# Turning x on VectorE and carrying it through DRAM at the stage boundaries of a two-layer encoder trunk

## The chip, the cores and the metric

The kernel runs on one core of one Trainium2 chip, in one launch. The metric is the device time of the whole program in microseconds (us). Engines are named as in the profile: PE is TensorE's matmul, PEld its weight load, DVE is VectorE, ACT is ScalarE, POOL is GpSimd, SP is SyncE, which here issues nearly all DMAs from one queue, in order.

## The reference

The model is a trunk of two layers over x of shape (1, 256, 1024) in float32, with a memory of 256 x 1024. Cut to what matters here:

```python
for i in range(2):
    x = x + 0.5 * swiglu(rmsnorm(x, ffn1_norm[i]), ffn1_w_gate[i], ffn1_w_up[i], ffn1_w_down[i])
    h = rmsnorm(x, mix_norm[i])
    q_s, k_s, v_s, q_m = split(h @ w_in[i])              # 768, 768, 768, 256 columns
    k_m, v_m = split(rmsnorm(mem, mem_norm[i]) @ w_mem_kv[i])
    o_m = memory_attention(...)                          # 4 heads of 64 over 256 memory rows
    o_s = chunked_rel_attention(...) if i == 0 else diff_attention(...)   # 12 heads, or 6 pairs of heads
    x = x + concat(o_s, o_m) @ w_out[i]
    x = x + 0.5 * swiglu(rmsnorm(x, ffn2_norm[i]), ffn2_w_gate[i], ffn2_w_up[i], ffn2_w_down[i])
# swiglu(h) = (silu(h @ w_gate) * (h @ w_up)) @ w_down, with w_gate, w_up 1024 x 2816 and w_down 2816 x 1024
```

## The kernel before, in words

**Stages.** Feed-forward 1, mixer, feed-forward 2, twice: six stages with five boundaries between them. x stays in SBUF as two blocks of 128 tokens (`xs[tb]`, `tb` 0 and 1), each handled in two halves of 512 columns (`hf`).

**Arithmetic.** A float32 product is made of three matmuls in a reduced form: every operand is split into hi (a rounded copy, ScalarE) and lo (the rest, VectorE), and `dense` (lines 370 to 393) issues hi x hi (L383), x hi x weight lo (L386) and x lo x weight hi (L389), each 128 x 128 by 512 columns. One call of `dense` is three matmuls.

**Weights.** They come in chunks of 128 x 2048 float32 (1 MB). `loader` fills `raw` buffers (three), `split_hi` (L302) and `split_lo` (L314) split them by quarters of 512 columns into hi and lo buffers (four of each, `NHL`). A raw buffer is free again when lo is made, a hi/lo pair when all eight `dense` calls on the chunk are done. A gate/up group of a feed-forward stage has two chunks, one for each half of the 1024 inputs; there are 11 groups. Each `w_down` chunk serves 256 of the 2816 inner columns; there are 11 of these too.

**x for the next stage.** `prep_half` makes from a half of x the turned, gain-multiplied operands: TensorE turns four 128 x 128 squares into a PSUM tile (`xtp`, `turn`, L396), VectorE multiplies by the norm's gain (`y`, L427), ScalarE makes hi (`xh`, L430), VectorE lo (`xl`, L432). The sum of squares runs beside it (`square`, L441); the factor it gives is applied after the matmuls. `finish` (from L460) adds the stage's result to x (L466 after feed-forward, L469 after a mixer) and calls `prep_half`, half after half, for one block.

**Feed-forward.** `ffn` runs the gate/up groups; `evac` takes each group's result: silu on ScalarE (L491), the product on VectorE (L494), and then turns it for the down product without TensorE: VectorE turns 32 x 32 squares (L503, two instructions for each block and group), SP writes the tile `hb` to a DRAM tile `hd` (L508) and reads it back in four pieces in the other block order (`hr`, L514); hi and lo follow (L521, L523). The down product keeps four PSUM banks (2 blocks x 2 halves). The first 8 of 11 chunks (`SPLIT = NG - 3`) run chunk by chunk over all four banks; the last three run bank by bank, so that block 0 half 0 is complete first, then block 0 half 1, block 1 half 0, block 1 half 1, and `finish` can begin on the early ones. I call these four stretches the tail's quarters.

**Order of the groups.** Group 0 of a stage (but the very first) runs block 0 with both chunks and then block 1; later groups run chunk by chunk, with both blocks on each.

**Mixer.** `proj` runs five projections, each block 0 then block 1: q and k of four heads, v (512 columns), q and k twice more, and last the rest of v with the memory's queries. Eight attention units (`unit`) run beside them as their inputs come. The output product has four chunks, two run chunk by chunk, two bank by bank as above. Before the first mixer the memory is prepared (`memory_prep`, started in the first feed-forward stage after down chunk 6: TensorE turns `mtp`, ScalarE L630, VectorE L635), and its key/value projections for both layers (`memory_kv`) run ahead of the mixer's own.

**Who sets the order.** The order on every engine and queue is fixed when the program is written, by a planner (`Flow`) with its own clock and cost for each instruction. A piece of work is a generator that yields the planned time at which its next step is ready. The two weight splits are idle work: they get in where the planner believes the engine to be free within 0.4 us, or when TensorE has already come to the chunk:

```python
yield lambda: flow.free["A"] <= flow.now + SLACK or i <= at[0] + AHEAD
```

At run time the engines follow that order and wait on semaphores; an instruction that waits holds up everything behind it on its engine or queue.

## Time and profile before

| | |
|---|---|
| time, median of 3 | 975.2 us (974.78 to 975.77) |
| profiled execution | 975.12 us, span from first to last instruction 973.3 us |
| granted TensorE clock | 1.00 throughout |
| busy, share of the span | PE 99%, PEld 81%, DVE 69%, ACT 56%, POOL 6% |
| DMA | 200.9 MB, mean 206 GB/s |
| turns of x on TensorE (xtp, L396) | 96 in 24 groups of four, 280 ns each |
| turns of the activations on VectorE (L503) | 176, 289 ns each |

A row of the groups of instructions reads: line, engine, operation, output<-inputs, shapes, xcount | busy us, mean ns. A row of the timeline or of an engine's list reads: start us, duration us, engine, line, operation, output<-inputs, count, and in brackets the idle time of the engine before it and what ended that. A row of the stretches reads: from:to, length, then for each of PE, PEld, DVE, ACT and POOL the busy us and instruction count, granted clock, DMA share, GB/s. PE's busy time has modelled ends; the starts of the weight loads (PEld) show TensorE's pace.

First matmuls of the stages behind the five boundaries: memory projections 193.77, feed-forward 2 320.57, feed-forward 1 of layer two 502.02, the second mixer between 683 and 684.2, feed-forward 2 of layer two 789.12 us.

### The profile page before, as it was taken

How to read it: one execution, taken by the hardware profiler on the slowest of the kernel's cores; microseconds unless marked ns; L12 is line 12 of the kernel's file. 1: busy time of each engine (PE TensorE's matmuls, PEld its weight loads, DVE VectorE, ACT ScalarE, POOL GpSimd, SP SyncE). 2: the span in 40 equal slices, each digit the busy share in tenths (PEclk: the TensorE clock that was granted, in tenths of full speed). 3: DMA queues.
4: the chain of work that ended last, by engine and by line, in shares of the span. 5: the costliest groups of instructions: out<-in, count | busy, mean ns of one | idle time of the engine just before them, and what ended most of it. 6: DMA issues, size and time to landing. Idle time of an engine off the chain costs nothing.

```text
span 973.3 us, 13393 instructions
## 1 busy us (share of the span) xinstructions
PE 964.6 (99%) x4576; PEld 791.3 (81%) x4576; DVE 675.7 (69%) x1485; ACT 542.4 (56%) x1159; POOL 60.1 (6%) x65
## 2 busy tenths in 40 slices
PE   9999999999999999999999999999999999999998
PEld 7888888887777888888888888888787788888886
DVE  6776675887777866666476676644989886676641
ACT  6554544766685655445445555443677764555540
POOL 0000000022210000000000000000344100000000
PEclk9999999999999999999999999999999999999999
DMA  9989766475525567887648887764641369788641
GB/s 289 306 242 270 257 225 206 162 260 173 174 87 173 163 209 223 242 263 242 235 124 252 250 252 237 253 207 136 207 140 50 125 199 284 235 251 254 226 130 44
DMA packets 164447, 200.90 MB, mean 206 GB/s; under 512 B 9433, under 2 KB 140058, under 8 KB 164378
## 3 DMA queue, kind: packets, MB, share of 16 engines
q1 hardware_dynamic: 164378, 200.04, 65.5%
q8 instruction: 36, 0.59, 0.3%
q14 instruction: 33, 0.27, 0.1%
HBM read 187.42 MB, written 12.58 MB: 205 GB/s over the span
## 4 chain that ended last, share of the span: by engine, by line
PE 91%; DVE 5%; ACT 1%; DMA 1%; issue 0%; SPq 0%; ACTq 0%
PE gu L383 16%; PE gu L386 16%; PE gu L389 16%; PE acc L386 9%; PE acc L389 9%; PE acc L383 9%; PE pj L389 3%; PE pj L383 3%; PE pj L386 3%; DVE lo L314 2%; PE xtp L396 1%; PE S L983 1%; PE AV L1064 1%; PE kv L389 1%; PE kv L386 1%; PE kv L383 1%
## 5 line engine op out<-in xcount | busy, mean ns | idle before, releaser
L314 DVE TENSOR_TENSOR lo<-raw,hi 128x512 fp32r<-128x512 f32 x656 | 416.5, 684 | 161.5 <-ACT hi L302 161.3
L302 ACT CAST hi<-raw 128x512 fp32r<-128x512 f32 x656 | 365.4, 618 | 241.3 <-PE gu L389 117.9
L389 PE MATMUL gu<-hi,xl 128*128 128x512 f32 x704 | 274.3, 390 | 0.0
L383 PE MATMUL gu<-hi,xh 128*128 128x512 f32 x704 | 274.1, 389 | 0.0
L386 PE MATMUL gu<-lo,xh 128*128 128x512 f32 x704 | 274.0, 389 | 0.0
L389 PEld LDWEIGHTS gu<-hi,xl 128*128 128x128 f32 x704 | 132.2, 188 | 27.5
L383 PEld LDWEIGHTS gu<-hi,xh 128*128 128x128 f32 x704 | 132.2, 188 | 27.3
L386 PEld LDWEIGHTS gu<-lo,xh 128*128 128x128 f32 x704 | 132.2, 188 | 27.2
L383 PE MATMUL acc<-hi,ht 128*128 128x512 f32 x352 | 137.7, 391 | 0.0
L386 PE MATMUL acc<-lo,ht 128*128 128x512 f32 x352 | 137.3, 390 | 0.2 <-DVE lo L314 0.2
L389 PE MATMUL acc<-hi,ht 128*128 128x512 f32 x352 | 137.4, 390 | 0.0
L386 PEld LDWEIGHTS acc<-lo,ht 128*128 128x128 f32 x352 | 66.1, 188 | 14.1 <-DVE lo L314 0.7
L389 PEld LDWEIGHTS acc<-hi,ht 128*128 128x128 f32 x352 | 66.1, 188 | 13.7
L383 PEld LDWEIGHTS acc<-hi,ht 128*128 128x128 f32 x352 | 66.1, 188 | 13.5
L523 DVE TENSOR_TENSOR ht<-hr,ht 128x512 fp32r<-128x512 f32 x44 | 30.3, 688 | 55.0 <-ACT ht L521 55.0
L521 ACT CAST ht<-hr 128x512 fp32r<-128x512 f32 x44 | 27.1, 617 | 69.5 <-DMA hr<-hd 69.5
L389 PE MATMUL pj<-hi,xl 128*128 128x512 f32 x160 | 64.6, 404 | 0.0
L386 PE MATMUL pj<-lo,xh 128*128 128x512 f32 x160 | 63.6, 398 | 0.0
L383 PE MATMUL pj<-hi,xh 128*128 128x512 f32 x160 | 63.6, 398 | 0.0
L491 ACT ACTIVATE sil<-gu,xr 128x256 f32<-128x256 f32 x88 | 41.4, 470 | 17.5 <-PE gu L389 17.5
L503 DVE STREAM_TRANSPOSE hb<-h 128x128 f32<-128x128 f32 x176 | 44.1, 289 | 1.2
L494 DVE SCALAR_TENSOR_TENSOR h<-gu,xr,sil 128x256 f32<-128x256 f32 x88 | 42.2, 480 | 1.6
(167 smaller groups left out, 806.5 us busy)
## 6 DMA issues: line engine op xcount, KB each, us to landing
raw<-in_ffn_w_down_dram SPq DMA_DIRECT2D x44, 1024.0 KB
raw<-in_ffn_w_gate_dram SPq DMA_DIRECT2D x86, 512.0 KB
raw<-in_ffn_w_up_dram SPq DMA_DIRECT2D x86, 512.0 KB
raw<-in_w_in_dram SPq DMA_DIRECT2D x32, 512.0 KB
hd<-hb SPq DMA_DIRECT2D x44, 256.0 KB
hr<-hd SPq DMA_DIRECT2D x176, 64.0 KB
raw<-in_w_out_dram SPq DMA_DIRECT2D x8, 1024.0 KB
raw<-in_w_mem_kv_dram SPq DMA_DIRECT2D x4, 1024.0 KB
```

Of the source, the lines that this page charges most:

```text
L302: nc.scalar.copy(out=c.hi[:, sl], in_=c.raw[:, sl])
L314: nc.vector.tensor_sub(c.lo[:, sl], c.raw[:, sl], c.hi.bitcast(F32)[:, sl])
L383: nc.tensor.matmul(out=ps, lhsT=xh, rhs=wh, start=start, stop=False)
L386: nc.tensor.matmul(out=ps, lhsT=xh, rhs=wl, start=False, stop=False)
L389: nc.tensor.matmul(out=ps, lhsT=xl, rhs=wh, start=False, stop=stop)
L396: nc.tensor.transpose(out=dst, in_=src, identity=flip if flipped else ident)
L491: nc.scalar.activation(sil, ps[tb][:, 0:256], AF.Silu, scale=xt.r[tb])
L494: nc.vector.scalar_tensor_tensor(out=h, in0=ps[tb][:, 256:512], scalar=xt.r[tb], in1=sil, op0=ALU.mult, op1=ALU.mult)
L503: nc.vector.transpose(out=hb[:, :, f, tb, :], in_=h[:, f * P:(f + 1) * P])
L521: nc.scalar.copy(out=hi, in_=src)
L523: nc.vector.tensor_sub(lo, src, hi.bitcast(F32))
L983: nc.tensor.matmul(out=ss[e][:, pr, :nk], lhsT=q[rows, pr, :], rhs=k[rows, pr, :], start=i == 0, stop=i == len(passes) - 1)
```

## The change

**x's road.** `prep_half` has a second branch, `far`: VectorE turns the half in 32 x 32 squares (four instructions, `xb`), the new helper `through_dram` writes the tile to DRAM and reads it back in four pieces (`xr`), and the multiply by the gain reads `xr` from SBUF in the order that finishes the turn. `evac` uses the same helper for the activations. All four halves go this way after a feed-forward stage that has a successor, and block 1's two halves after a mixer; block 0 after a mixer and the start of the program stay on TensorE. With `far`, a block's first half is prepared as a piece of work of its own beside `finish`.

**Order.** The tail of a down product takes four chunks (`SPLIT = NG - 4`). The first two groups of every feed-forward stage but the first run block by block: block 0 of groups 0 and 1, then block 1 of both. The second mixer does the same with its first q/k projection and v. The very first group runs input square by input square with both blocks.

**Start and end.** x of block 1, first half, is loaded before the first weights, and the planner's start times move. The last stage's result leaves in pieces of 256 columns, from SP's and ScalarE's queues in turn.

```diff
@@ -187,6 +187,7 @@
                           in_=x[0, tb * P:(tb + 1) * P, hf * 512:(hf + 1) * 512])
 
     load_x(0, 0)
+    load_x(1, 0)
 
     ident = const.tile([P, P], F32, name="ident")
     make_identity(nc, ident)
...
@@ -414,18 +412,46 @@
             self.rt = [None, None]
             self.done = [0, 0]
 
-    def prep_half(xt, tb, hf, gc, wait=0.0):
-        yield banks.has()
-        tp = bank("xtp")
-        for k in range(4):
-            t = turn(tp[:, k, :], xs[tb][:, hf * 512 + k * P:hf * 512 + (k + 1) * P])
-        yield t
+    def through_dram(src, name):
+
+        d = dram.tile([4, 32, 4, P], F32, tag="hd", name="hd")
+        nc.sync.dma_start(out=d.rearrange("a i b x -> (a i) (b x)"), in_=src)
+        yield flow.now + 3.2
+        g2.give()
         yield g2.has()
-        y = g2.take([P, 4, P], F32, "y")
+        r = g2.take([P, 4, P], F32, name)
+        for b in range(4):
+            nc.sync.dma_start(out=r[32 * b:32 * b + 32], in_=d[:, :, b, :].rearrange("a i x -> i a x"))
+        yield flow.now + 4.0
+        return r
+
+    def prep_half(xt, tb, hf, gc, wait=0.0, far=False):
         ks = slice(hf * 4, hf * 4 + 4)
         g = gcol[:, gc + hf * 4:gc + hf * 4 + 4]
-        nc.vector.tensor_tensor(out=y, in0=tp, in1=g.unsqueeze(2).broadcast_to([P, 4, P]), op=ALU.mult)
-        banks.give()
+        if far:
+            yield g2.has(2)
+            xb = g2.take([P, 4, 4, 32], F32, "xb")
+            for k in range(4):
+                nc.vector.transpose(out=xb[:, :, k, :], in_=xs[tb][:, hf * 512 + k * P:hf * 512 + (k + 1) * P])
+                t = flow.dve(128, 0.05)
+            yield t
+            xr = yield from through_dram(xb.rearrange("p b k j -> p (b k j)"), "xr")
+            yield g2.has()
+            y = g2.take([P, 4, P], F32, "y")
+            nc.vector.tensor_tensor(out=y.rearrange("p k (a j) -> p k a j", a=4),
+                                    in0=xr.rearrange("p a (k j) -> p k a j", k=4),
+                                    in1=g.unsqueeze(2).unsqueeze(3).broadcast_to([P, 4, 4, 32]), op=ALU.mult)
+            g2.give()
+        else:
+            yield banks.has()
+            tp = bank("xtp")
+            for k in range(4):
+                t = turn(tp[:, k, :], xs[tb][:, hf * 512 + k * P:hf * 512 + (k + 1) * P])
+            yield t
+            yield g2.has()
+            y = g2.take([P, 4, P], F32, "y")
+            nc.vector.tensor_tensor(out=y, in0=tp, in1=g.unsqueeze(2).broadcast_to([P, 4, P]), op=ALU.mult)
+            banks.give()
         yield flow.dve(512)
         nc.scalar.copy(out=xt.h[tb][:, ks, :], in_=y)
         yield flow.act(512)
@@ -457,11 +483,20 @@
             self.ps = [[bank(f"acc{tb}{hf}", (P, 512)) for hf in range(2)] for tb in range(2)]
             self.t = [[None, None], [None, None]]
 
-    def finish(acc, tb, xt, gc, half):
+    def finish(acc, tb, xt, gc, half, far):
         for hf in range(2):
             sl = slice(hf * 512, (hf + 1) * 512)
             yield lambda: acc.t[tb][hf] is not None
             yield acc.t[tb][hf]
+            if xt is None:
+                for q in range(2):
+                    qs = slice(hf * 512 + q * 256, hf * 512 + q * 256 + 256)
+                    nc.vector.scalar_tensor_tensor(out=xs[tb][:, qs], in0=acc.ps[tb][hf][:, q * 256:q * 256 + 256],
+                                                   scalar=0.5, in1=xs[tb][:, qs], op0=ALU.mult, op1=ALU.add)
+                    yield flow.dve(256)
+                    (nc.scalar if q else nc.sync).dma_start(out=out[0, tb * P:(tb + 1) * P, qs], in_=xs[tb][:, qs])
+                banks.give()
+                continue
             if half:
                 nc.vector.scalar_tensor_tensor(out=xs[tb][:, sl], in0=acc.ps[tb][hf], scalar=0.5, in1=xs[tb][:, sl],
                                                op0=ALU.mult, op1=ALU.add)
@@ -469,10 +504,10 @@
                 nc.vector.tensor_add(xs[tb][:, sl], acc.ps[tb][hf], xs[tb][:, sl])
             banks.give()
             yield flow.dve(512)
-            if xt is None:
-                nc.sync.dma_start(out=out[0, tb * P:(tb + 1) * P, sl], in_=xs[tb][:, sl])
+            if far and hf == 0:
+                flow.spawn(prep_half(xt, tb, hf, gc, far=True))
             else:
-                yield from prep_half(xt, tb, hf, gc)
+                yield from prep_half(xt, tb, hf, gc, far=far)
 
 
     def ffn(l, nm, xt, gc_next):
@@ -503,20 +538,11 @@
                     nc.vector.transpose(out=hb[:, :, f, tb, :], in_=h[:, f * P:(f + 1) * P])
                     t = flow.dve(128, 0.05)
                 g2.give()
-            hd = dram.tile([4, 32, 4, P], F32, tag="hd", name="hd")
-            yield t
-            nc.sync.dma_start(out=hd.rearrange("a i b x -> (a i) (b x)"), in_=hb.rearrange("p b f t j -> p (b f t j)"))
-            yield flow.now + 3.0
-            g2.give()
-            yield g2.has()
-            hr = g2.take([P, 4, 2, 2, 32], F32, "hr")
-            for b in range(4):
-                nc.sync.dma_start(out=hr[32 * b:32 * b + 32].rearrange("p a f t j -> p a (f t j)"),
-                                  in_=hd[:, :, b, :].rearrange("a i x -> i a x"))
-            yield flow.now + 4.0
+            yield t
+            hr = yield from through_dram(hb.rearrange("p b f t j -> p (b f t j)"), "hr")
             yield g4.has()
             ht = g4.take([P, 2, 4, P], F32R, "ht")
-            src = hr.rearrange("p a f t j -> p (f t) a j")
+            src = hr.rearrange("p a (c j) -> p c a j", c=4)
             hi, lo = (ht[:, i].rearrange("p c (a j) -> p c a j", a=4) for i in range(2))
             nc.scalar.copy(out=hi, in_=src)
             yield flow.act(512)
@@ -525,20 +551,42 @@
             g2.give()
             hts[g], htt[g] = ht, t
 
-        for g, ids in enumerate(plan[l, nm, "gu"]):
+        def open_group(g):
             flow.until(banks.has(2))
-            ps = [bank(f"gu{tb}", (P, 512)) for tb in range(2)]
-            end = [None, None]
+            ps, end = [bank(f"gu{tb}", (P, 512)) for tb in range(2)], [None, None]
             flow.spawn(evac(g, ps, end))
-            order = [(tb, c) for tb in range(2) for c in range(2)] if g == 0 and (l, nm) != (0, 1) else \
-                    [(tb, c) for c in range(2) for tb in range(2)]
-            for tb, c in order:
-                for k in range(4):
-                    kk = 4 * c + k
-                    t = dense(ps[tb], xt.h[tb][:, kk, :], xt.l[tb][:, kk, :], lambda: xt.t[tb][kk], ids[c], k,
-                              lambda w: k4(w)[:, k, :], kk == 0, kk == KT - 1)
-                if c == 1:
-                    end[tb] = t
+            return g, ps, end
+
+        def run(grp, tb, kk):
+            g, ps, end = grp
+            c, k = kk // 4, kk % 4
+            t = dense(ps[tb], xt.h[tb][:, kk, :], xt.l[tb][:, kk, :], lambda: xt.t[tb][kk], plan[l, nm, "gu"][g][c], k,
+                      lambda w: k4(w)[:, k, :], kk == 0, kk == KT - 1)
+            if kk == KT - 1:
+                end[tb] = t
+
+        rest = 0
+        if (l, nm) == (0, 1):
+            grp = open_group(0)
+            for kk in range(KT):
+                for tb in range(2):
+                    run(grp, tb, kk)
+            rest = 1
+        else:
+            grps = []
+            for tb in range(2):
+                for g in range(2):
+                    if tb == 0:
+                        grps.append(open_group(g))
+                    for kk in range(KT):
+                        run(grps[g], tb, kk)
+            rest = 2
+        for g in range(rest, NG):
+            grp = open_group(g)
+            for c in range(2):
+                for tb in range(2):
+                    for k in range(4):
+                        run(grp, tb, 4 * c + k)
         flow.until(banks.has(4))
         acc = Acc()
         nxt = None if gc_next is None else Xt()
@@ -551,7 +599,7 @@
             return dense(acc.ps[tb][hf], ht[:, 0, 2 * k + tb, :], ht[:, 1, 2 * k + tb, :], lambda: htt[c], dn[c], 2 * k + hf,
                          lambda w: k2(w)[:, k, sl], c == 0 and k == 0, c == NG - 1 and k == 1)
 
-        SPLIT = NG - 3
+        SPLIT = NG - 4
         for c in range(SPLIT):
             for k in range(2):
                 for tb in range(2):
@@ -563,7 +611,7 @@
         if nm == 1:
             table_hint(AF.Exp)
         for tb in range(2):
-            flow.spawn(finish(acc, tb, nxt, gc_next, True))
+            flow.spawn(finish(acc, tb, nxt, gc_next, True, True))
             for hf in range(2):
                 for c in range(SPLIT, NG):
                     for k in range(2):
@@ -846,16 +894,19 @@
             for tb in range(2):
                 V[tb] = g4.take([P, 768], F32, f"V{tb}")
 
-        def proj(i, evac):
-            flow.until(banks.has(2))
-            ps = [bank(f"pj{tb}", (P, 512)) for tb in range(2)]
+        def proj(*parts):
+            pss = []
             for tb in range(2):
-                for c in range(2):
-                    for k in range(4):
-                        kk = 4 * c + k
+                for n, (i, evac) in enumerate(parts):
+                    if tb == 0:
+                        flow.until(banks.has(2))
+                        pss.append([bank(f"pj{j}", (P, 512)) for j in range(2)])
+                    ps = pss[n]
+                    for kk in range(KT):
+                        k = kk % 4
                         t = dense(ps[tb], xt.h[tb][:, kk, :], xt.l[tb][:, kk, :], lambda: xt.t[tb][kk],
-                                  plan[l, "in"][i][c], k, lambda w: k4(w)[:, k, :], kk == 0, kk == KT - 1)
-                flow.spawn(evac(ps[tb], tb, t))
+                                  plan[l, "in"][i][kk // 4], k, lambda w: k4(w)[:, k, :], kk == 0, kk == KT - 1)
+                    flow.spawn(evac(ps[tb], tb, t))
 
         class Heads:
             def __init__(self):
@@ -1202,13 +1253,18 @@
                 memory_kv(ll)
         for c, tb in ((0, 0), (0, 1), (1, 0), (1, 1), (2, 0), (3, 0), (2, 1), (3, 1)):
             flow.spawn(unit(c, tb))
-        proj(0, qk_evac(0))
-        flow.until(g4.has(2))
-        take_v()
-        proj(1, v_evac)
-        proj(2, qk_evac(1))
-        proj(3, qk_evac(2))
-        proj(4, vq_evac)
+        if typ_a:
+            proj((0, qk_evac(0)))
+            flow.until(g4.has(2))
+            take_v()
+            proj((1, v_evac))
+        else:
+            flow.until(g4.has(3))
+            take_v()
+            proj((0, qk_evac(0)), (1, v_evac))
+        proj((2, qk_evac(1)))
+        proj((3, qk_evac(2)))
+        proj((4, vq_evac))
 
         flow.until(banks.has(4))
         acc = Acc()
@@ -1232,7 +1288,7 @@
             g4.give()
         table = [False]
         for tb in range(2):
-            flow.spawn(finish(acc, tb, nxt, gc_next, False))
+            flow.spawn(finish(acc, tb, nxt, gc_next, False, tb == 1))
             for hf in range(2):
                 for i in range(2, 4):
                     for k in range(2):
...
```

13 lines of the change are left out of this document (5 added, 8 removed).

## The prediction

> **What bounds the kernel now.** I read the page first, then the stages, then the weight loads of TensorE (PEld) one by one.
>
> ```profile
> PE 964.6 (99%) x4576; PEld 791.3 (81%) x4576; DVE 675.7 (69%) x1485; ACT 542.4 (56%) x1159; POOL 60.1 (6%) x65
> PE 91%; DVE 5%; ACT 1%; DMA 1%; issue 0%; SPq 0%; ACTq 0%
> L396 PE MATMUL xtp<-ident,x 128*128 128x128 f32 x96 | 15.0, 280 | 0.9 <-DMA x<-in_x_dram 0.9
> ...
> 690.00:780.00 90.00, 87.82 (x502) 69.29 (x502) 81.25 (x184) 64.69 (x182) 30.89 (x27) 1.00 0.40 130
> ...
> 800.00:880.00 80.00, 80.00 (x354) 66.24 (x354) 54.60 (x112) 42.27 (x82) 0.00 (x0) 1.00 0.85 256
> ```
>
> TensorE is the bound: 91% of the chain of waits. In the stretch 800 to 880 it issues 354 matmuls in 80.00 us, one per 0.226 us, at a granted clock of 1.00. Only in the second mixer (690 to 780) is VectorE nearly as full (81.25 of 90 us). So what is taken off TensorE is gained whole, as long as nothing makes TensorE wait. What four turns of x cost on it:
>
> ```profile
> 489.23 0.19 PEld L386 LDWEIGHTS acc<-lo,ht 128*128 128x128 f32 x1
> 489.46 0.19 PEld L389 LDWEIGHTS acc<-hi,ht 128*128 128x128 f32 x1
> 489.68 0.59 PEld L396 LDWEIGHTS xtp<-ident,x 128*128 128x128 f32 x4
> 490.24 0.19 PEld L383 LDWEIGHTS acc<-hi,ht 128*128 128x128 f32 x1
> 490.35 0.19 PEld L386 LDWEIGHTS acc<-lo,ht 128*128 128x128 f32 x1
> ```
>
> Loads step by 0.23 us; without the turns L383 would start at 489.68 and L386 at 489.91. L386 starts at 490.35, so a group of four costs 0.44 us.
>
> **The change, part by part.** I write T0 for the first matmul of the next stage and call the last four quarters of a feed-forward stage Q1 to Q4 (block 0 halves 0, 1, block 1 halves 0, 1).
>
> *Removed.* Four groups at each of three feed-forward ends and two (block 1) at each of two mixer ends: 16 x 0.44 = 7.0 us less TensorE. The remaining eight of the 24 groups stay.
>
> *The new road of a half.* VectorE turns, SP writes and reads back.
>
> ```profile
> 510.55 0.50 DVE L503 STREAM_TRANSPOSE hb<-h 128x128 f32<-128x128 f32 x2
> ...
> 383.00 0.45 SPq L508 DMA_DIRECT2D hd<-hb  x1
> ...
> 448.75 0.34 SPq L508 DMA_DIRECT2D hd<-hb  x1
> ...
> 529.97 0.34 SPq L508 DMA_DIRECT2D hd<-hb  x1
> 532.80 1.75 SPq L514 DMA_DIRECT2D hr<-hd  x4
> ...
> 395.80 0.62 ACT L521 CAST ht<-hr 128x512 fp32r<-128x512 f32 x1 [6.16 <-DMA hr<-hd]
> 456.81 0.62 ACT L521 CAST ht<-hr 128x512 fp32r<-128x512 f32 x1 [3.64 <-DMA hr<-hd]
> 539.09 0.62 ACT L521 CAST ht<-hr 128x512 fp32r<-128x512 f32 x1 [2.03 <-DMA hr<-hd]
> ```
>
> Two turns take 0.50 us, four about 0.9. The activations already make the same trip with the same sizes: from the write's issue to the first use 8.1 us (448.75 to 456.81), 9.1 (529.97 to 539.09) and, at worst here, 12.8 (383.00 to 395.80). I take 9.1, from just after a stage start, where the new trips lie too. The read waits 2.8 us for the write (529.97 to 532.80), on SP itself; the weight loads queued behind it wait with it. [...]
>
> Feed-forward to feed-forward, T0 = 502.02:
>
> ```profile
> 484.67 2.18 ACT L302 CAST hi<-raw 128x512 fp32r<-128x512 f32 x4 [3.26 <-PE acc L389]
> 499.23 1.66 ACT L302 CAST hi<-raw 128x512 fp32r<-128x512 f32 x3 [2.14 <-PE acc L389]
> ...
> 500.27 1.89 DVE L314 TENSOR_TENSOR lo<-raw,hi 128x512 fp32r<-128x512 f32 x3
> 502.68 0.69 DVE L466 SCALAR_TENSOR_TENSOR x<-acc,x 128x512 f32<-128x512 f32 x1
> 503.28 1.89 DVE L314 TENSOR_TENSOR lo<-raw,hi 128x512 fp32r<-128x512 f32 x3
> 505.69 2.49 DVE L314 TENSOR_TENSOR lo<-raw,hi 128x512 fp32r<-128x512 f32 x4
> 508.69 0.69 DVE L314 TENSOR_TENSOR lo<-raw,hi 128x512 fp32r<-128x512 f32 x1
> 509.95 0.68 DVE L314 TENSOR_TENSOR lo<-raw,hi 128x512 fp32r<-128x512 f32 x1
> ...
> 502.02 0.19 PEld L383 LDWEIGHTS gu<-hi,xh 128*128 128x128 f32 x1
> ```
>
> The last half's x starts 0.66 us after T0 (502.68). Then x 0.69, turns 0.9, trip 9.1, and gain, hi and lo 0.69 + 0.62 + 0.69: 12.7 in all, ready at T0 + 13.4. It is first needed by block 1, second half, of group 0: after 2 x 24 + 12 = 60 matmuls, T0 + 13.6. So it is covered by 0.2 us; the earlier halves end 5.4 us (24 matmuls) apart and are needed at T0, T0 + 2.7 and T0 + 10.9, so the tightest of them has 0.2 us too (13.4 against 10.9 + 2.7). With the 12.8 us trip a boundary would lose 3.5 us.
>
> *What block by block asks.* Groups 0 and 1 are now both wanted by block 0 in the first 48 matmuls: 16 weight quarters by T0 + 10.2 (the 45th matmul), where before eight were wanted by T0 + 4.8. And with four chunks instead of three in the written-out tail, all four split buffers are held until Q4: the next stage's first chunk, now split early (the row at 484.67), waits for the first six matmuls of Q4, that is until T0 - 4.1. Before, 12 quarters and the other VectorE work ran from 500.27 to 510.63, 10.4 us, to T0 + 8.6. Added: four quarters at the 0.60 us step of the row of three (2.4), the last turns (0.9), gain and lo of Q2, which now come back late (1.3); gone to later: the same two of the last half (1.3). The start moves 1.4 us ahead (Q4 has 24 matmuls now, not 18). That is 13.7 us from T0 - 3.1 to T0 + 10.6: 0.4 late; ScalarE's hi and the fourth chunk's load behind SP's wait can add to it. I take 0.8 us at this boundary and 0.8 at the one into the second mixer; bounds 0 (slack of VectorE used earlier) and 2.5 each.
>
> At the mixers' ends two chunks can be split early as before and only block 1 travels; but x is late there:
>
> ```profile
> 789.12 0.19 PEld L383 LDWEIGHTS gu<-hi,xh 128*128 128x128 f32 x1
> ...
> 792.14 0.69 DVE L469 TENSOR_TENSOR x<-acc,x 128x512 f32<-128x512 f32 x1
> ```
>
> That is T0 + 3.0, which makes the half ready at T0 + 15.7: 2.1 us late, less if x no longer queues behind the other half's work, which now comes later. I take 0.9 there and 0.6 at the first mixer's end; bounds 0 and 2.
>
> *The first feed-forward end* is followed by the memory projections, so x's trips are free there. But the tail is:
>
> ```profile
> 168.15 1.03 PEld L396 LDWEIGHTS mtp<-ident,raw 128*128 128x128 f32 x8
> ...
> 169.01 3.03 ACT L630 ACTIVATE memh<-mtp,gcol 128x256 fp32r<-128x256 f32 x8 [2.32 <-PE mtp L396]
> 172.41 3.17 ACT L630 ACTIVATE memh<-mtp,gcol 128x256 fp32r<-128x256 f32 x8 [0.36 <-PE mtp L396]
> 175.60 1.28 ACT L576 ACT_TABLE_LOAD   x1
> 177.00 4.25 ACT L302 CAST hi<-raw 128x512 fp32r<-128x512 f32 x8
> ...
> 174.01 3.26 DVE L635 SCALAR_TENSOR_TENSOR meml<-mtp,gcol,memh 128x256 fp32r<-128x256 f32 x8 [0.17 <-ACT memh L630]
> 177.64 1.29 DVE L314 TENSOR_TENSOR lo<-raw,hi 128x512 fp32r<-128x512 f32 x2 [0.36 <-ACT hi L302]
> ...
> 179.69 0.19 PEld L386 LDWEIGHTS acc<-lo,ht 128*128 128x128 f32 x1 [0.67 <-DVE lo L314]
> ```
>
> When chunk 6 is done (168.15), the memory's preparation starts and the buffer of down chunk 10 comes free. Its split is written behind memh and meml, since the planner lets a split in only where it believes the engine idle; TensorE already waits 0.67 us for it. Before, chunk 7 still ran whole first; now the four-chunk tail starts at once and asks for chunk 10 after 18 matmuls and the 16 memory turns (1.8 us): 168.15 + 4.1 + 1.8 = 174.0. VectorE is at meml until 177.27, so the first quarter comes at about 177.9 and the third (next needed) 1.2 later, against 0.7 of matmuls: 3.9 + 0.5 - 0.7 = **3.7 us** lost. Bounds: 0, if the planner puts the split between the memory's pieces, and 5, if the table load now stands ahead of all of it and delays it.
>
> *Second mixer.* Its order is block 0 of q/k and v, then block 1. VectorE has 8.75 us free in the 90 us row; the moved quarters (2.4) and turns (0.9) fill some of it. I take 0.6; bounds -1 and 3.
>
> [...]
>
> *Start and end.*
>
> ```profile
> 8.59 0.66 PE xtp L396 x4
> 969.57 0.69 DVE x L466
> ```
>
> TensorE's first matmuls waited for x of block 1, now loaded before the weights; the weights then come 256 KB later. I take 0, bounds -1 and 1. At the end two halves of 0.69 us work leave in turn: 0, bounds -0.5 and 0.5.
>
> **Sum:** -7.0 + 3.7 + 0.8 + 0.8 + 0.6 + 0.9 + 0.6 = +0.4 us on the profiled 975.12 (span 973.3 and 1.8 around it; the median is 975.2): **975.5 us**.
>
> **Rivals.** *A: all of it is covered.* Chunk 10 gets in between the memory's pieces, and the 3.7 vanish: 971.8. For it: VectorE is free for 31% of the span, and the memory's pieces arrive in bursts. Against it: the 0.67 us wait seen already, and an order fixed beforehand. *B: the trip is longer than its cover.* Place: block 1, second half, groups 0 and 1 (or q/k and v), at four boundaries. It decides from a trip of some 10.1 us (9.3, and the 0.8 already counted as lost gives room); at 11.5, between 9.1 and the 12.8 seen, each loses 1.4 more: 975.5 + 5.6 = 981. For it: SP holds up reads and weight loads in one queue. Against it: most of the quoted trips are shorter. *C: the second mixer is VectorE's.* q/k of block 1 come 24 matmuls (5.4 us) later, its attention starts later, and VectorE first lacks work and then has too much; with 3 us of it at the stage's end: 978.5. Against it: VectorE's total there hardly grows.
>
> **Chances:** forecast 0.38 (itself 973.5 to 977), A 0.34, B 0.13, C 0.15. A measurement of this kernel can tell about 0.2%, 2 us, from no change: faster 0.34, same 0.38, slower 0.28. The range 968.5 to 980.5 reaches over A with the other terms at their lower bounds (-3.1 more) and over C, up to B.
>
> **What will show it.** No xtp turns at the three feed-forward ends; 32 instead of 96 in all. In the first tail, a TensorE wait of 4 us on lo of chunk 10: its absence is A. At T0 + 5 to T0 + 11 of the third and fourth boundary, short waits on lo; waits on xl there mean B. A longer stretch from first q/k to last attention in the second mixer means C. I am wrong in principle if TensorE's pace without turns is not 0.226 us, or if fewer than 7 us of its work are gone.

## The result: 2.7% slower

The changed kernel takes 1001.0 us (median; 999.0 to 1006.6) against 974.9 (974.4 to 975.8): a ratio of 1.027 [1.024, 1.030]. The forecast was 975.5, with a range to 980.5. The profiled execution has a span of 999.0 us against 973.3, 25.7 more.

From the profile of the changed kernel: busy times, shares of the chain of waits, the group of x's turns, and two stretches (busy us of PE, PEld, DVE, ACT and POOL with their counts, granted clock, DMA share, GB/s).

```profile
PE 969.4 (97%) x4520; PEld 790.6 (79%) x4520; DVE 687.5 (69%) x1553; ACT 541.2 (54%) x1159; POOL 60.0 (6%) x65
PE 76%; DVE 10%; DMA 9%; ACT 2%; SPq 2%; issue 1%; DVEq 0%; ACTq 0%
L394 PE MATMUL xtp<-ident,x 128*128 128x128 f32 x32 | 4.8, 277 | 0.1
700.00:790.00 90.00, 83.41 (x445) 65.90 (x444) 82.93 (x184) 62.63 (x174) 30.45 (x27) 1.00 0.48 149
850.00:890.00 40.00, 40.00 (x179) 33.10 (x178) 26.49 (x56) 20.66 (x42) 0.00 (x0) 1.00 0.79 238
```

The turns are gone as predicted: 32 instead of 96. Undisturbed, TensorE keeps its pace: 178 weight loads in 40.00 us. But its share of the chain has fallen from 91% to 76%, and what came in is DVE (5 to 10%) and DMA (1 to 9%).

Where the time went, from the first weight load of each stage in the two traces; the last column is what the terms of the prediction put there:

| stretch, us | before | after | change | predicted |
|---|---|---|---|---|
| start and first gate/up | 130.1 | 133.4 | +3.3 | 0 |
| first down product | 63.7 | 67.4 | +3.7 | +1.9 |
| memory projections | 23.0 | 28.1 | +5.1 | 0 |
| mixer 1, projections | 71.4 | 71.4 | 0 | 0 |
| mixer 1, output | 32.4 | 31.9 | -0.5 | -0.9 |
| gate/up behind mixer 1 | 120.2 | 124.7 | +4.6 | +0.6 |
| down product | 61.3 | 59.8 | -1.5 | -1.8 |
| gate/up of layer two | 120.1 | 124.4 | +4.3 | +0.8 |
| down product | 61.3 | 59.8 | -1.5 | -1.8 |
| mixer 2 | 105.7 | 109.5 | +3.8 | +0.5 |
| gate/up behind mixer 2 | 120.2 | 124.6 | +4.4 | +0.9 |
| last down product and end | 64.0 | 63.9 | -0.1 | 0 |

The gain shows in the tails. It is given back, about three times over, at the beginning of every stage that receives x.

**One such boundary, from mixer 2 to its feed-forward** (first matmul T0 = 810.55). Rows of the timeline of the changed kernel: start, us, engine, line, operation, tiles, count, in brackets idle time and its releaser.

```profile
814.45 0.38 SPq L418 DMA_DIRECT2D hd<-xb  x1
814.92 0.40 SPq L271 DMA_DIRECT2D raw<-in_ffn_w_gate_dram  x1
...
817.90 0.51 SPq L271 DMA_DIRECT2D raw<-in_ffn_w_up_dram  x1
818.51 1.86 SPq L424 DMA_DIRECT2D xr<-hd  x4
826.22 0.69 DVE L441 TENSOR_TENSOR y<-xr,gcol 128x512 f32<-128x512 f32 x1 [6.66 <-DMA xr<-hd]
826.95 0.62 ACT L456 CAST xh<-y 128x512 fp32r<-128x512 f32 x1 [7.61 <-DVE y L441]
827.62 0.29 PEld L381 LDWEIGHTS gu<-hi,xh 128*128 128x128 f32 x1 [3.15 <-ACT xh L456]
828.21 0.48 DVE L529 SCALAR_TENSOR_TENSOR h<-gu,xr,sil 128x256 f32<-128x256 f32 x1
828.64 0.33 PEld L381 LDWEIGHTS gu<-hi,xh 128*128 128x128 f32 x1
```

Block 1's last half is written at 814.45; between write and read four loads of 512 KB of weights are issued (814.92 to 817.90), and y starts at 826.22: a trip of 11.8 us, not 9.1. TensorE stands for 3.15 us, on exactly the operand that rival B named. (Behind mixer 1 it stands for 3.35 us, on the half before that one.) While y waits 6.66 us at the head of VectorE's queue, the product h of the running group stands behind it (828.21). And weight loads that take 0.19 us take 0.33 afterwards.

The same road with no weight load issued beside it, in the tail ahead of the third boundary:

```profile
502.59 0.34 SPq L418 DMA_DIRECT2D hd<-xb  x1
504.91 1.75 SPq L424 DMA_DIRECT2D xr<-hd  x4
508.30 0.69 DVE L441 TENSOR_TENSOR y<-xr,gcol 128x512 f32<-128x512 f32 x1 [0.29 <-DMA xr<-hd]
```

That is 5.7 us. The DMA engines move 132 GB/s in these 5.7 us, and 237 GB/s in the 11.8 us above. At this boundary (T0 = 516.84) TensorE does not wait for an operand made of x, but for the lo of a weight chunk:

```profile
513.95 0.34 SPq L418 DMA_DIRECT2D hd<-xb  x1
522.32 0.19 PEld L381 LDWEIGHTS gu<-hi,xh 128*128 128x128 f32 x1
524.34 0.69 DVE L441 TENSOR_TENSOR y<-xr,gcol 128x512 f32<-128x512 f32 x1 [2.34 <-DMA xr<-hd]
524.95 2.49 DVE L312 TENSOR_TENSOR lo<-raw,hi 128x512 fp32r<-128x512 f32 x4
525.69 0.19 PEld L384 LDWEIGHTS gu<-lo,xh 128*128 128x128 f32 x1 [3.18 <-DVE lo L312]
```

The weights are there: TensorE uses the hi of this chunk at 522.32. Its lo stands on VectorE behind the y of block 1's first half, whose trip takes 10.4 us (513.95 to 524.34), and TensorE goes on when the first lo ends. So it is again x that is late, through VectorE's queue. At the fourth boundary it is the same: y at 707.13 and 714.02 waits 0.88 and 1.18 us for xr, the lo behind it starts at 707.74 and 714.63, and TensorE loses 1.73 and 1.84 us.

**In the memory projections** nothing of TensorE needs x yet, but VectorE waits for it all the same:

```profile
209.10 0.69 DVE L441 TENSOR_TENSOR y<-xr,gcol 128x512 f32<-128x512 f32 x1 [3.07 <-DMA xr<-hd]
214.46 0.48 DVE L640 SCALAR_TENSOR_TENSOR kmn<-kv,mr,hf 128x256 f32<-128x256 f32 x1
214.99 0.20 PEld L394 LDWEIGHTS kmtp<-ident,kmn 128*128 128x128 f32 x2 [2.98 <-DVE kmn L640]
```

The memory's keys (kmn) come behind the y that waits and the splits that it pushed back, and TensorE's turn of them loses 2.98 us.

**The first tail and the start**, from the same timeline:

```profile
79.09 0.14 PEld L231 LDWEIGHTS gps<-ident,grow 55*128 55x128 f32 x1 [2.33 <-issue]
80.25 0.33 PEld L381 LDWEIGHTS gu<-hi,xh 128*128 128x128 f32 x1
...
177.37 3.26 DVE L683 SCALAR_TENSOR_TENSOR meml<-mtp,gcol,memh 128x256 fp32r<-128x256 f32 x8 [0.18 <-ACT memh L678]
180.10 0.19 PEld L381 LDWEIGHTS acc<-hi,ht 128*128 128x128 f32 x1 [2.74 <-ACT hi L300]
180.78 0.69 DVE L312 TENSOR_TENSOR lo<-raw,hi 128x512 fp32r<-128x512 f32 x1
181.52 0.19 PEld L384 LDWEIGHTS acc<-lo,ht 128*128 128x128 f32 x1 [1.23 <-DVE lo L312]
182.78 0.29 PEld L384 LDWEIGHTS acc<-lo,ht 128*128 128x128 f32 x1 [0.74 <-DVE lo L312]
```

Chunk 10 is waited for as predicted, behind memh and meml: 2.74 + 1.23 + 0.74 = 4.7 us, against 0.67 before. Not predicted is the first row: the turn of the gain columns (gps), whose small loads now come later, stands in TensorE's queue for 2.33 us.

**Half clock.** The granted clock in stretches of the changed kernel, and the first of them before:

```profile
75.00:90.00 15.00, 13.06 (x51) 10.29 (x50) 9.38 (x24) 5.83 (x11) 0.00 (x0) 0.89 0.92 269
820.00:835.00 15.00, 12.27 (x48) 9.65 (x47) 6.99 (x15) 6.33 (x14) 0.56 (x1) 0.89 0.41 121
```

```profile
75.00:90.00 15.00, 15.00 (x67) 12.11 (x66) 9.96 (x23) 8.42 (x17) 0.00 (x0) 1.00 0.95 269
```

After each of the six waits of 2.3 us and more (2.33 to 3.35), five to eight matmuls step by up to 0.43 us, not 0.227; behind the wait that ends at 827.62 the granted clock is 0.50 up to 830.80. Over the trace these are 40 steps, 40 x 0.2 = some 8.0 us; before there is none. TensorE's waits, summed over the list of what its weight loads waited for, are 45.6 us after and 18.9 before: 26.7 more. With 8.0 of half clock and 7.0 of turns saved that is +27.7, where 25.7 were measured; the last 2 us are not assigned.

### The profile page after: what moved, and what is told of

Same layout as the page of the kernel before. It is cut to its first block, busy times and chain, and to the rows that moved or that the text cites. A ratio compares the mean times of both kernels' runs of the same rounds, so it can differ in the third digit from the quotient of the medians.

```text
span 999.0 us, 13486 instructions
## 1 busy us (share of the span) xinstructions
PE 969.4 (97%) x4520; PEld 790.6 (79%) x4520; DVE 687.5 (69%) x1553; ACT 541.2 (54%) x1159; POOL 60.0 (6%) x65
## 4 chain that ended last, share of the span: by engine, by line
PE 76%; DVE 10%; DMA 9%; ACT 2%; SPq 2%; issue 1%; DVEq 0%; ACTq 0%
PE gu L387 13%; PE gu L384 13%; PE gu L381 13%; PE acc L387 9%; PE acc L384 9%; PE acc L381 9%; DVE lo L312 4%; DMA xr<-hd 3%; DMA raw<-in_ffn_w_up_dram 2%; PE pj L381 2%; PE pj L384 2%; PE pj L387 2%; DMA hr<-hd 2%; SPq L424 1%; ACT hi L300 1%
## 5 line engine op out<-in xcount | busy, mean ns | idle before, releaser
L381 PE MATMUL gu<-hi,xh 128*128 128x512 f32 x704 | 277.0, 393 | 5.7 <-ACT xh L456 5.7
L384 PE MATMUL pj<-lo,xh 128*128 128x512 f32 x160 | 63.9, 399 | 3.5 <-DVE lo L312 3.5
L381 PE MATMUL pj<-hi,xh 128*128 128x512 f32 x160 | 63.9, 400 | 0.0
L456 ACT CAST xh<-y 128x512 fp32r<-128x512 f32 x24 | 14.7, 618 | 72.1 <-DVE y L441 62.0
L526 ACT ACTIVATE sil<-gu,xr 128x256 f32<-128x256 f32 x88 | 41.3, 470 | 11.8 <-PE gu L387 11.7
```

Source lines behind the costliest of these rows:

```text
L381: nc.tensor.matmul(out=ps, lhsT=xh, rhs=wh, start=start, stop=False)
L384: nc.tensor.matmul(out=ps, lhsT=xh, rhs=wl, start=False, stop=False)
L456: nc.scalar.copy(out=xt.h[tb][:, ks, :], in_=y)
L526: nc.scalar.activation(sil, ps[tb][:, 0:256], AF.Silu, scale=xt.r[tb])
```

## The experiments

Two theories stood at the start: the road of x itself is the loss (late x, late weights, VectorE held), or the things changed around it (tail of four chunks, start, block by block order) are. In the expectations W (later W2) stands for the first, that weight loads make x late, and S for a part of the second, that the block by block order asks for too many splits at once (16 weight quarters in 48 matmuls). All edits are made on the changed kernel. The kernel before took 975.0 to 975.4 us beside them.

**x on TensorE, all else as changed.**

```diff
-finish(acc, tb, nxt, gc_next, True, True)
+finish(acc, tb, nxt, gc_next, True, False)
-finish(acc, tb, nxt, gc_next, False, tb == 1)
+finish(acc, tb, nxt, gc_next, False, False)
```

> The changed kernel with every half of x turned on TensorE again; the block-by-block order, the four-chunk tail, the start and the end stay. Theory W: the 7.0 us of turns come back and all waits at the stage starts go (some 4.4 us in each of three gate/up stages, 5.1 in the memory projections, 2.7 in the second mixer, 1.1 in its output product, less what the turns are in these): 1001 + 7 - 21 = 987. Theory S: the waits on lo at the third and fourth boundary stay, and with them 8 to 10 us: 995 to 998.

985.7 us, 1.010 [1.008, 1.012]. So carrying x costs 15.3 us net of the 7.0 it saves. In the stages that receive x two waits over 2 us are left, 2.1 us on the memory's keys and 2.6 us in the second mixer's attention. Behind the third and fourth boundary nothing is lost (120.1 and 104.8 us, against 120.1 and 105.7 before): the lo that I had feared there is not late when x is not carried.

**x on TensorE, tail of three chunks, old start.** What is left of the change is the block by block order and the pieces at the end.

```diff
-SPLIT = NG - 4
+SPLIT = NG - 3
...
-    load_x(1, 0)
-dma_free = [4.0]
+dma_free = [2.3]
```

> The changed kernel with x on TensorE, three chunks in the tail and the old start: of the change only the block-by-block order and the two-queue end are left. Theory W2: the order itself costs nothing, 974 to 977. Theory S: 979 to 983, with waits on lo in the first 11 us of the stages.

975.9 us, 1.001 [1.000, 1.002]. Order and end cost some 0.6 us; tail and start together cost 985.7 - 975.9 = 9.8 us. By stages these are 4.3 us at the start, 4.8 in the first down product and 1.9 in the memory projections; the later tails of four chunks cost nothing as long as x is not carried.

**The same, with x carried.**

> x travels as in the changed kernel, but the tail takes three chunks and the start and first group are those of before: against the run with x on TensorE, the three-chunk tail and the old start (975.9 us) only x's road differs. If the road itself is the loss (trips of 10 us and more under weight loads, waits of about 3 us, each followed by half clock), the time is 975.9 + 12 to 17, that is 988 to 993 us, with waits of 2 us or more at three or more stage starts. If the road is only dear together with the four-chunk tail and the new start, it is under 980 us. The theory of saved turns alone would give 975.9 - 7.0 = 969 us.

989.1 us, 1.014 [1.011, 1.016]: 13.2 us more than without the carrying, inside the 12 to 17 expected. The saved 7.0 are in it, so the road costs some 20 us gross, without the new tail and start. The waits lie otherwise than expected: over 1.5 us there are two at stage starts, both on xh behind mixer 1, one of 4.7 us on the memory's keys, and one of 2.9 us in the second mixer's attention. By stages, the memory projections take 7.2 us more than without the carrying, the gate/up stage behind mixer 1 5.4, the later ones 0.5 to 1.4.

**Tail of three chunks alone.**

> The changed kernel with a tail of three down chunks again. My prediction's term: the wait for down chunk 10 in the first tail (2.7 + 1.2 + 0.7 us and some 1.2 us of half clock) shrinks to the 0.6 us of before: 5 us less, 996. Theory W says the halves now follow each other in 4.1, not 5.4 us, so the trips of the last halves have the same cover but crowd more: up to 3 us given back, 996 to 999.

993.0 us, 1.018 [1.016, 1.021], 8.0 less than the changed kernel. The waits on chunk 10 shrink to one of 0.67 us and half clock to 24 steps. The 8.0 us are not the first tail alone, since the number of chunks holds for all tails: the first down product falls by 5.1 us and the memory projections rise by 3.6, and the stages behind the three later boundaries fall by 2.9, 3.5 and 3.0. Without x carried the later tails cost nothing, so this second part is tail and late x together; how, no run separates.

**Old start alone.**

> The changed kernel with the old start: load order of x, planner's start times, and the very first group chunk by chunk. If the new start is what makes TensorE wait 2.3 us at 76.6 us for the late gain loads (before: 0.34 us), that wait and the half clock after it (1.6 us) go, and the first matmul is 1.0 us later again: 998. If the wait has another cause, the time is 1002.

1002.6 us, 1.028 [1.025, 1.032]. The wait for the gain columns is gone and the first gate/up stage is back at 121.0 us, but stage by stage the 3 us gained are lost again in layer two, where TensorE waits 2.4 and 3.1 us for lo at the third boundary, both times behind a y that waits for xr. As long as the boundaries have no slack, an earlier gain need not last.

**Old order, x carried.**

```diff
-                for g in range(2):
+                for g in range(1):
...
-        if typ_a:
+        if True:
```

> The changed kernel with the old group order: block 0 then block 1 of group 0 alone, later groups chunk by chunk, and q/k before v in the second mixer. Theory W2 (the trip under weight loads takes 10 to 13 us, and what waits is x itself): block 1 is wanted 5.4 us earlier, so each of the four stage starts waits up to 5.4 us more: 1001 + 10 to 20 = 1011 to 1021. Theory S (16 quarters in 48 matmuls): the waits on lo at 522 and 706 us go, 992 to 996.

1010.6 us, 1.036 [1.032, 1.039]. TensorE waits 6.9 us for x behind mixer 1. So the new order does give cover, worth some 9.5 us here, just under the 10 expected; the cover is only too short.

**x by GpSimd's queue.** If SP's one queue were what makes the trips long, a queue of their own would shorten them.

```diff
-xr = yield from through_dram(xb..., "xr")
+xr = yield from through_dram(xb..., "xr", nc.gpsimd)
```

> The changed kernel with x's trip (one write, four reads per half) issued from GpSimd's queue, not from SP's. Theory W (weights in the way): in the changed kernel the reads of x stand behind up to 2 MB of weight loads in SP's queue (write at 814.45, reads at 818.51, use at 826.22), and SP's wait for the write holds weight loads up. Then trips of 11 to 13 us become 7 to 9, the waits of TensorE at 342.9 and 824.3 (3.3 and 3.1 us, each with some 1.4 us of half clock behind it) go, and the time falls from 1001 to 985 to 992. Theory S (splits): the waits come from 16 weight quarters asked for in 48 matmuls; then 1000 to 1002. If GpSimd is slow at issuing, trips get longer and the time rises above 1003.

1003.6 us, 1.029 [1.024, 1.033]. Timeline, behind mixer 2:

```profile
816.60 0.56 POOL L419 DMA_DIRECT2D hd<-xb  x1
823.38 2.21 POOL L425 DMA_DIRECT2D xr<-hd  x4 [5.43 <-issue]
828.58 0.69 DVE L442 TENSOR_TENSOR y<-xr,gcol 128x512 f32<-128x512 f32 x1 [5.39 <-DMA xr<-hd]
829.97 0.19 PEld L381 LDWEIGHTS gu<-hi,xh 128*128 128x128 f32 x1 [4.25 <-ACT xh L457]
```

12.0 us against 11.8: the length is not that of the queue, for the other queue saved nothing. Why it did not, no run here shows.

**Longer trips in the planner.** The written order puts y where the planner expects xr, 3.2 + 4.0 us after the write. With 4.5 + 7.0 VectorE should not be held.

```diff
-        yield flow.now + 3.2
+        yield flow.now + tw     # 4.5 for x
...
-        yield flow.now + 4.0
+        yield flow.now + tr     # 7.0 for x
```

> The changed kernel with only the planner's times for x's trip changed, from 3.2 + 4.0 to 4.5 + 7.0 us, so that the multiply by the gain is written later into VectorE's queue. If the loss comes from that multiply standing at the head of VectorE's queue (23.5 us of such waits) with ready work behind it, the waits in the memory projections (2.9 and 1.3 us) and on lo go, and x's own lateness at two mixer ends stays: 988 to 992. If x's lateness alone counts: 999 to 1002.

1012.5 us, 1.038 [1.036, 1.040]: a miss, slower instead of faster. VectorE waits less for xr (14.2 us in all instead of 23.5), but y comes later still. TensorE waits for xh at four boundaries (4.15, 3.82, 3.45 and 4.59 us), and 6.8 us for the memory's keys. Writing y later only moves the lateness from VectorE's queue to x itself.

**No weight load while a trip is under way.**

```diff
-            yield lambda: raw_left[0] > 0
+            yield lambda: raw_left[0] > 0 and trips[0] == 0
```

> The changed kernel, but no weight load is issued while the planner has a trip of x under way. Theory W2 (weights fill the DMA engines, whichever queue x uses): the trips shrink from 8 to 13 us to the 5.4 to 5.7 us that the quiet ones took (502.59 to 508.30), the waits on xh at 342.9 and 824.3 go, and waits for weights come in their place; the time is 990 to 1005. If the trips stay at 8 us or more, weights are not what lengthens them.

998.2 us, 1.023 [1.021, 1.025], 2.8 less. VectorE waits for xr 0.8 us in all, and the waits on xh behind both mixers are gone; those stages take 119.7 and 120.0 us. From write to y most trips still count 7.0 to 8.3 us, not the 5.4 to 5.7 expected, but y hardly waits any more: its place in the written order, 3.2 + 4.0 us after the write, sets it. In place of the waits on x, TensorE waits 3.6 us for hi of a weight chunk at the third boundary and, at the fourth, 6.4 us before the turn of q and k. With four chunks in the tail, holding the weights moves the lateness.

**The same with three chunks and the old start.**

> The same as the run with three chunks, old start and x carried, and no weight load is issued while a trip of x is believed under way. If traffic of weights on the DMA engines is what makes x late and nothing else were short, the time falls by most of the loss, to 975 to 980 us. If the boundary has no room for both (weights late instead of x), it falls by no more than 4 us: 985 to 991 us.

983.1 us (979.6 to 985.6), 1.007 [1.005, 1.010]: 6.0 less than without holding the weights, between the two bands expected. The trip of block 1's last half behind mixer 2, first with weight loads let in, then held back:

```profile
805.70 0.37 SPq L420 DMA_DIRECT2D hd<-xb  x1
806.91 0.39 SPq L270 DMA_DIRECT2D raw<-in_ffn_w_gate_dram  x1
809.87 1.75 SPq L426 DMA_DIRECT2D xr<-hd  x4
814.55 0.69 DVE L443 TENSOR_TENSOR y<-xr,gcol 128x512 f32<-128x512 f32 x1 [2.49 <-DMA xr<-hd]
```

```profile
797.18 0.38 SPq L421 DMA_DIRECT2D hd<-xb  x1
799.54 1.73 SPq L427 DMA_DIRECT2D xr<-hd  x4
803.80 0.68 DVE L446 TENSOR_TENSOR y<-xr,gcol 128x512 f32<-128x512 f32 x1
```

8.9 us and 6.6 us; the write alone holds the read up 4.2 and 2.4 us. And VectorE's whole wait for xr, from the list of waits (us in total, times, longest) of the two:

```profile
DVE y L443 <- DMA xr<-hd: 20.5, 9, 3.5
```

```profile
DVE y L446 <- DMA xr<-hd: 2.7, 2, 2.0
```

So it is the loads of the weights that make x late. What is left shows in one stage of this trace (the fastest run, 979.6 us): the memory projections take 28.8 us, against 23.0 with x on TensorE, and every other stage is within 1.4 us. There the memory's keys are still late (1.66 and 1.53 us), and holding costs too: the last chunk of memory weights is issued at 203.39 us, not among the three from 180.27 on as before, and TensorE waits 1.31 us for its hi.

**Only block 0, only after feed-forward stages.** These four-chunk tails (three chunks in the first) leave the trip in the tail, where the one at 502.59 met no weight load (132 GB/s).

```diff
-finish(acc, tb, nxt, gc_next, True, True)
+finish(acc, tb, nxt, gc_next, True, tb == 0)
...
-SPLIT = NG - 4
+SPLIT = NG - (3 if (l, nm) == (0, 1) else 4)
```

> Only block 0's halves travel, only at the three feed-forward ends; all mixer ends and block 1 are turned on TensorE; the first tail has three chunks, the others four; the start is the old one. Six groups of turns are saved, 6 x 0.44 = 2.6 us, against the 975.9 us of the run in which none travels. If lateness alone makes the road dear, these six trips (most of them inside the tail, where no weights move, 5.4 to 5.7 us each) are covered: 972.5 to 975 us, with no wait on xh over 1 us. If the road costs in itself (SP held by the read's wait, VectorE's turns, weights issued later), it is 977 to 984 us, with waits on lo of the first chunks at the second and third boundary.

979.8 us, 1.004 [1.002, 1.005]. In the band of a road that costs in itself, but not at the place named there. The memory projections take 27.6 us, not 23.0, and the only wait of TensorE over 2 us is in them:

```profile
195.47 0.69 DVE L443 TENSOR_TENSOR y<-xr,gcol 128x512 f32<-128x512 f32 x1 [3.69 <-DMA xr<-hd]
197.28 0.68 DVE L503 SCALAR_TENSOR_TENSOR x<-acc,x 128x512 f32<-128x512 f32 x1
198.01 0.71 PEld L396 LDWEIGHTS xtp<-ident,x 128*128 128x128 f32 x4 [3.43 <-DVE x L503]
```

y waits for xr, block 1's x stands behind it on VectorE, and TensorE's turn behind that. This first trip takes 12.0 us (183.49 to 195.47): at this end the memory's weights are being loaded beside it.

**The same without the first end, in the old order.**

```diff
+finish(acc, tb, nxt, gc_next, True, tb == 0 and (l, nm) != (0, 1))
```

> The order and the start of before; block 0's halves alone travel, at the second and third feed-forward ends alone, with a tail of four chunks there. Four groups of turns are saved, 4 x 0.44 = 1.8 us. In the run in which block 0 also travelled at the first end, the only wait over 2 us was there: y waited 3.69 us for xr at the head of VectorE's queue, block 1's x stood behind it, and TensorE's turn behind that (3.43 us). If lateness alone makes the road dear, that wait is gone and the time is 975.2 - 1.8, with 0.6 for the changed end and order gone too: 972.5 to 974.2 us. If the road has a price of its own of 0.4 us and more a half, it is 975 us or more.

974.2 us (973.7 to 976.0), 0.9986 [0.9977, 0.9995], 1.0 us under the kernel before, where 1.8 were saved. Its first trip, and the stage behind mixer 1:

```profile
486.28 0.34 SPq L420 DMA_DIRECT2D hd<-xb  x1
488.66 1.75 SPq L426 DMA_DIRECT2D xr<-hd  x4
492.04 0.69 DVE L443 TENSOR_TENSOR y<-xr,gcol 128x512 f32<-128x512 f32 x1 [0.34 <-issue]
...
320.00:441.00 121.00, 121.00 (x538) 100.20 (x537) 87.73 (x204) 67.60 (x131) 2.01 (x2) 1.00 0.78 236
```

5.8 us, in time, and no matmul steps at half clock anywhere.

**Weights held, three chunks, old start, and x on TensorE behind the first feed-forward stage.**

```diff
+finish(acc, tb, nxt, gc_next, True, (l, nm) != (0, 1))
```

> The run with weights held, three chunks and the old start (983.1 us; span 977.8), but behind the first feed-forward stage x is turned on TensorE. In that run's trace the memory projections take 28.8 us against 23.0 with x on TensorE, and every other stage is within 1.4 us. If that one boundary is where the rest of the loss lies, the time falls by 5.8 less the 1.8 of turns that come back, to 977 to 979.5 us by the medians. If the rest is spread over the boundaries, it stays at 981 us or more.

976.4 us, 1.0015 [1.0001, 1.0029]: 6.7 us less than with that boundary, and the memory projections take 23.0 us again. The rest of the loss against the kernel before was there, and a little more of it than expected. It is still no gain, though 12 groups of turns (5.3 us) are gone. Behind the second and third feed-forward stage TensorE waits eight times, 0.5 to 1.0 us, for xh or xl of block 0, 2.9 and 3.2 us in all: with a tail of three chunks block 0 is done nearer to the next stage, and its x is late.

**Quiet trips and held weights only.** Block 0 as in the run of 974.2 us, block 1 at the mixers' ends, block by block order behind the mixers alone, weights held.

> Block 0's halves travel at the second and third feed-forward ends with a tail of four chunks there (974.2 us alone), and block 1's two halves at both mixer ends, with the block by block order behind the mixers only and weight loads held during a trip. Four more groups of turns are saved, 1.8 us. In the run with weights held the stages behind both mixers had no wait on xh and lost nothing (119.7 and 119.9 us against 120.2). If late x was all that made the mixer ends dear, the time is 972 to 974 us. If holding the weights only moves the lateness, it is 975 us or more, with waits on hi or lo behind the mixers.

973.2 us (971.3 to 975.9), 0.9971 [0.9962, 0.9981]. This is 0.2 to 0.4% under the kernel before: small, but clear of the noise. From its list of waits and its timeline behind mixer 2, and the stretch that holds this boundary:

```profile
DVE y L446 <- DMA xr<-hd: 3.8, 3, 1.8
...
790.05 0.37 SPq L421 DMA_DIRECT2D hd<-xb  x1
793.89 1.73 SPq L427 DMA_DIRECT2D xr<-hd  x4
797.38 0.69 DVE L446 TENSOR_TENSOR y<-xr,gcol 128x512 f32<-128x512 f32 x1 [1.84 <-DMA xr<-hd]
...
790.00:820.00 30.00, 30.00 (x134) 24.86 (x133) 21.09 (x44) 16.91 (x35) 1.49 (x2) 1.00 0.80 246
```

The trip is 7.3 us, TensorE is busy throughout at full clock. Eight groups of turns are gone, 8 x 0.44 = 3.5 us; 2.2 of them arrive in the median, and all in the profiled execution (971.7). Lateness, then, was nearly the whole price of the road: where the trips are quiet or kept quiet, and covered, carrying x gains.

## Why the prediction was wrong

- **The turns (-7.0): right.** 64 of 96 are gone, and the stretches with nothing but the turns removed, the two later down products, are 1.5 us shorter each (1.8 priced).
- **The trip (9.1 us, covered by 0.2): the step that failed.** Nothing was missing for it: the same section held 8.1, 9.1 and 12.8 us for the same transfer and I took the middle one, though x travels at the one moment when the loader refills for the next stage. None of the three was quiet: beside each of them 2 MB of weight loads are issued (beside the 8.1 at 449.93 and 452.89), and beside the longest 1 MB more just ahead of the write (380.99 and 381.43). In the changed kernel the trips that were waited for took 10.4 to 14.2 us with 2 MB of loads issued beside them, and the quiet ones 5.4 and 5.7. Cover of 0.2 us meant that any of this is lost. Behind the mixers, where I put 0.9 and 0.6, TensorE waited 3.1 and 3.3 us.
- **Two readings on the way to it.** I read the 2.8 us from write to read (529.97 to 532.80) as a wait on SP; two weight loads go out in between (531.15 and 531.56), so the wait is 0.7 us. And at the mixers' ends I looked at the last half alone. The halves are written only 2.9 us apart there (332.16 and 335.04), so by the same sum block 1's first half is ready at T0 + 12.8 and wanted at T0 + 10.9, as late as the last; behind mixer 1 TensorE waited for that one.
- **The trips at the first feed-forward end (0, "free there"): wrong.** TensorE does not need x there, but VectorE waits for it ahead of the memory's keys: +5.1 us, and 6.7 us are gained in the run with weights held when x is turned on TensorE at this end alone.
- **Rival B** named the mechanism and, behind mixer 2, the operand, but its price, 5.6 us for four boundaries, was about a quarter of the 20 us that the road cost at five. It counted x's own lateness only. Left out were what waits behind y on VectorE (the memory's keys, and lo at the third and fourth boundary), and half clock.
- **Half clock: unseen.** The trace of before does not show it: the clock is 1.00 throughout, and the longest wait is 1.3 us at the start and 1.0 later. Every lateness was priced at its own length; in the changed kernel each of the six waits of 2.33 to 3.35 us cost 1.0 to 1.6 us more in slow steps.
- **Lo at the boundaries (0.8 and 0.8): right in place, wrong in reason and size.** The waits on lo came, 5.5 us behind T0 at both and 12.2 at the fourth, but not from the amount of work: with x on TensorE and the same order and tails, nothing is lost there. lo stands behind a y that waits for xr, and TensorE lost 3.2 us at the one and 1.7 and 1.8 at the other.
- **First tail (3.7): right in place, cause and size.** 4.7 - 0.7 = 4.0 us of waits, the first of them on hi, with half clock behind them; with x on TensorE tail and half clock together cost 4.8 us in this stage. The 8.0 of its undoing hold other boundaries too.
- **Second mixer (0.6, with 0.8 at its boundary):** +3.8 for the whole stage, with 3.6 us of waits on lo behind y. Rival C, the order itself, is ruled out: with the same order and x on TensorE the stage takes 104.8 us, against 105.7 before.
- **Start (0, bounds -1 and 1): wrong.** TensorE starts 1.0 us earlier and loses 2.3 us and half clock at 79 us, on a small load moved behind others. I had looked at x and the weights, and not at what else stands in that queue.

With every term at its own bound the sum would run from 965.6 to 986.6 us (the stated range left some of the bounds out), still far from 1001.0: the terms failed, not the adding up. Why the errors had one sign: three terms of the sum stood on covers of a few tenths of a microsecond, and each was costed as if the others kept theirs.

What stays open: which resource the weights and x share (the DMA engines or the memory behind them) was not separated, nor what a tail of four chunks adds to a late x in layer two; and 2 us of the sum of waits have no place.

## What to carry to other kernels

Price a transfer by rows from the traffic that it will meet, and where its cover is thin by the longest of them: here the same 512 KB of moving cost 5.7 us quiet and 12 beside weight loads, from SP's queue and from GpSimd's. A stall of TensorE is to be counted with what it does to the clock (1.0 to 1.6 us behind each of the six above), and a wait put at the head of an in-order queue with everything behind it (y waited 3.07 us for xr, and TensorE then 2.98 us for the memory's keys). Moving work off the bound engine gains only where the data come back with slack to spare; kept to such places it gained 0.3%, taken everywhere it lost 1.4%, and 2.7% with the new tail and start.

## What the runs showed of the hardware

- **Behind most waits of 3 us TensorE ran at half clock.** In the 16 traces, 26 of the 29 waits of 2.9 us or more are followed within 4 us by four or more matmuls at 0.43 us a step; of the 24 between 2.2 and 2.9 us 15 are followed by at least three; and of the 19 between 1.5 and 2.2 us one, with a second wait of 1.3 us right behind it. It is not the length alone: the six waits of 2.6 to 3.0 us ahead of the attention's turns (ptp) are followed by none. The step is nearly twice 0.227, and the granted clock behind the wait that ends at 827.62 is 0.50. In the changed kernel the shortest wait with slow steps behind it is 2.33 us (79.09 above), the longest without them 1.84 (715.37). What sets it beside the length, no run shows.
- **The round trip through DRAM** of 256 KB took 5.4 to 5.8 us quiet, 6.6 and 7.3 with no new load between write and read, and 10.4 to 14.2 in the changed kernel where x was waited for beside weight loads of 2 MB. Three trips ahead of the second mixer took 6.5 to 7.6 us with no load issued beside them; why, no run shows.
